# The down product of a gated feed-forward as seven block products in a stage of its own, and gate and up summed in PSUM banks that were read

## The chip, the cores and the metric

One Trainium2 chip, and of it one NeuronCore: TensorE (PE in the profile; its weight loads are PEld), VectorE (DVE), ScalarE (ACT), GpSimd (POOL) and SyncE (SP), which issues the kernel's DMAs. The metric is the device time of one execution in microseconds, the median of the runs shown.

## The reference

A hybrid encoder layer for 1536 tokens (512 of one sequence, 1024 of another) of width 1024: a token mixer, a cross attention to 256 memory rows of each sequence, and a gated feed-forward with a hidden width of 2816, each between RMS norms with a residual. The change lies in the last part:

```python
def swiglu(h, w_gu, w_down):
    gu = h @ w_gu
    gate, up = gu[..., :D_FF], gu[..., D_FF:]
    return (jax.nn.silu(gate) * up) @ w_down
...
    ff = swiglu(rms_norm(x, nw[NORM_PRE_FFN]), ffn_w_gu, ffn_w_down)
    return x + rms_norm(ff, nw[NORM_POST_FFN])
```

## The kernel before, in words

All large products are made in three terms: each fp32 factor is split into a high part and a rest (`split`, L135: ScalarE writes the high part, L136, VectorE the rest, L137), and `mm3` (L156 to L159) issues high x high, high x rest and rest x high into one PSUM bank. Each of these is one matmul with a weight load of its own.

Stages: column products and the mixer (to L518), memory (L521), projections back (L562), cross attention (L662), a second projection (L901), then the feed-forward (L907 to L1040), which the change concerns. The tokens stand in two groups of 768. In a group, gate and up are made for 11 pairs of tiles of the hidden width: `q` counts 44 steps, `g, r = divmod(q, 22)`, `p, up = divmod(r, 2)`; even q are gate, odd q up. Each q is a product of 2x2 blocks in Winograd's form: seven block products (`step` 0 to 6) in place of eight. A block product is four `mm3`, so 12 matmuls of 384 columns. The token side (`S`, seven factors for a group, in the order `NAMES`) stays in SBUF for the whole group; those of the second group wait in DRAM (`sd`) and are loaded and split at q = 21 (L1011 to L1015), through two slots `s_land`.

The weight side of a step is a factor `TS[q, step]`. `load_raw` (L863) loads the weights of a q, `sums` (L871) makes four sums of their blocks on GpSimd, and `make_T` (L882) splits one factor after each product. Five are made ahead; they lie in a ring of five slots, `t_r`.

After each product its PSUM bank is read into SBUF tiles of 384 columns `c[11]`, `c[12]`, `c[21]`, `c[22]` (L973 to L992): one copy by ScalarE (L975) and seven sums by VectorE (L978 to L992; step 5 frees its bank with L989). Every product has a bank of its own from a ring of four (`mm`), and starts it anew. Gate results go through Silu on ScalarE (L995), up results are multiplied by them on GpSimd (L997).

The down product (`down`, L914) is plain and stands among the steps: after steps 2, 4 and 6 of each q from 2 to 41 it takes one tile of 128 tokens of the pair before, 12 matmuls of 512 columns into two `sm` banks, and adds them to `acc` in SBUF (L926, L928). Hidden rows and down weights are split at the end of each up q (L1031 to L1034). `final` (L931) normalises a tile, adds the residual `x2d` and writes it out; the first group's tiles are finished during p = 0 of the second group (L1016 to L1022, L1035). A last loop (L1038) makes the down products of the last two pairs and finishes the second group.

The order on each engine follows the program in the main, but not line by line: the compiler lays out each engine's instructions, and one that is ready can be placed ahead of one that is not. Each engine then runs its own list in that order. All DMAs go through SP's list.

Of the kernel before, what the change touches and what calls it, by code (L numbers as in the profile page):

```python
# [17 lines left out]
P = 128  # L18
# [17 lines left out]
class Part:  # L36
    """Units of a kilo-element per partition in tiles of three units."""
# [30 lines left out]
def carve(units, *specs):  # L68
    """Cut rings of (width, count) out of units, first fit."""
# [13 lines left out]
def encoder_kernel(ctx: ExitStack, tc, x, xTp, xTs, mem, memT, norm_w, w_in, lg, small, sgu_nw, sgu_wT,  # L83
# [72 lines left out]
    def mm3(ps, a, b, first, last):  # L156
        T.matmul(ps, lhsT=a[0], rhs=b[0], start=first, stop=False)  # L157
        T.matmul(ps, lhsT=a[0], rhs=b[1], start=False, stop=False)  # L158
        T.matmul(ps, lhsT=a[1], rhs=b[0], start=False, stop=last)  # L159
# [20 lines left out]
    # Work of one step is emitted in pieces, so that it runs between pieces of the large products.  # L180
# [32 lines left out]
    def xTk(k, t):  # L213
        """hi and lo of x^T (times the norm weight) for k tile k and token tile t."""
# [6 lines left out]
    def load_pairs(src, n):  # L221
        """Two k tiles of a transposed input, times norm weight n."""
# [76 lines left out]
    # the rows of the memory: rsqrt of the mean square, as a column and as a row on all partitions  # L299
# [15 lines left out]
    def chunk_tiles(c, tiles, post):  # L315
        """z of column chunk c for the token tiles; post(i, t, ps) makes the generator that uses it."""
# [22 lines left out]
    # spatial gating  # L339
# [41 lines left out]
    # retention  # L381
# [8 lines left out]
    for h in range(4):  # L390
# [5 lines left out]
        # dec: q forward, k forward, k backward, q backward, whole chunk forward, backward  # L396
# [6 lines left out]
    def ret_tile(h, c, n, t, ps, pk, rf):  # L403
# [5 lines left out]
        # rotary on q and k  # L409
# [160 lines left out]
    def transposed(tiles, n, out, part):  # L570
        """Units of two k tiles: hi and lo of the transposed rows of four token tiles, times norm weight n."""
# [12 lines left out]
    def project(src, w, n_post, res, dst, groups, a_r, xt_r, stat, use, ahead):  # L584
        """dst = res + norm(src^T @ w); use(i, tiles) makes the generator that uses the rows of group i."""
# [541 lines left out]
```

## Time and profile before

| | |
|---|---|
| Time of three runs | 2123.74, 2123.78, 2125.71 us, median 2123.78 |
| Span of the profiled execution | 2124.7 us (no other time of this execution is shown) |
| TensorE busy, share | 98% |
| Feed-forward, first gate matmul to the end | 1088.9 to 2124.7 us |
| Mean granted TensorE clock | 0.996 of full speed |

The span runs from the first to the last instruction; it lies 0.9 us above the median of the runs. Busy times of TensorE are those of pipelined matmuls that overlap, with ends that are modelled, so distances between starts say more. In a timeline row stand the start, the duration, the engine, the line, the operation, out<-in by tile names, the shapes and the count, and in brackets the idle time of the engine before it and what ended it.

### The profile page before, as it was taken

The numbers are of one execution on the slowest core, as the hardware profiler recorded it, in microseconds if no ns is written. First come the engines' busy times: TensorE is split into PE (matmuls) and PEld (weight loads), VectorE is DVE, ScalarE is ACT, GpSimd is POOL, SyncE is SP. The second block draws the span as 40 slices with busy tenths as digits, with TensorE's granted clock in tenths as the row PEclk, the third lists the DMA queues.
The fourth block names the chain that finished last, engine by engine and source line by source line (L and its number), as shares of the span: only waits on it lengthen the run. The fifth ranks groups of instructions, "written<-read, shape, count | busy, mean of one in ns | idle before, by whom it ended". The sixth has DMA issues, their size and how long they took to land.

```text
span 2124.7 us, 28590 instructions
## 1 busy us (share of the span) xinstructions
PE 2087.0 (98%) x10640; PEld 1842.9 (87%) x10640; DVE 1233.0 (58%) x2447; ACT 794.6 (37%) x1588; POOL 565.4 (27%) x537
## 2 busy tenths in 40 slices
PE   8899999999999999999999999999998999999998
PEld 7787888888788888888889999999997999999996
DVE  4235566575423554455666666666678566666666
ACT  7522222234324443444454333333344433333332
POOL 0122222221022200003344233333335433333333
PEclk9999999999999999999999999999999999999999
DMA  8311101024733422243473222122244321221213
GB/s 329 109 39 58 46 16 48 28 66 133 225 102 129 158 71 70 70 139 119 149 212 100 74 76 70 60 70 70 62 160 141 119 70 60 70 70 62 88 50 119
DMA packets 84618, 207.55 MB, mean 98 GB/s; under 512 B 9344, under 2 KB 34560, under 8 KB 84480
## 3 DMA queue, kind: packets, MB, share of 16 engines
q1 hardware_dynamic: 84480, 205.73, 29.7%
q8 instruction: 84, 1.38, 0.3%
q14 instruction: 54, 0.44, 0.1%
HBM read 164.53 MB, written 41.16 MB: 97 GB/s over the span
## 4 chain that ended last, share of the span: by engine, by line
PE 85%; DVE 4%; issue 2%; DMA 2%; POOL 2%; ACT 1%; POOLq 0%; DVEq 0%; ACTq 0%
PE mm L157 17%; PE mm L159 17%; PE mm L158 17%; PE mm L625 12%; PE sm L159 6%; PE sm L158 5%; PE sm L157 5%; POOL rs L172 1%; DVE ra L137 1%; PE sm L578 0%; PE sm L731 0%; PE sm L362 0%; DMA fa<-in_wv_dram 0%; PE sm L818 0%; PE sm L446 0%
## 5 line engine op out<-in xcount | busy, mean ns | idle before, releaser
L136 ACT ACTIVATE ra<-ra 128x512 fp32r<-128x512 f32 x154 | 95.4, 631 | 339.6 <-PE mm L158 180.8
L157 PE MATMUL mm<-rc,ra 128*128 128x384 f32 (+1 forms) x592 | 203.4, 344 | 5.1 <-DVE rb L989 5.1
L158 PE MATMUL mm<-rc,ra 128*128 128x384 f32 (+1 forms) x592 | 202.9, 343 | 0.0
L159 PE MATMUL mm<-rc,ra 128*128 128x384 f32 (+1 forms) x592 | 202.6, 342 | 0.0
L159 PE MATMUL sm<-fb,rb 128*128 128x512 f32 x504 | 199.2, 396 | 1.8 <-DVE rb L137 1.8
L157 PE MATMUL sm<-fb,rb 128*128 128x512 f32 x504 | 196.7, 390 | 1.8 <-ACT fb L136 1.6
L157 PE MATMUL mm<-rx,ra 128*128 128x384 f32 (+1 forms) x512 | 185.1, 362 | 5.9 <-ACT rx L136 5.9
L997 POOL TENSOR_TENSOR rb<-rb 128x384 f32<-128x384 f32 x88 | 116.0, 1337 | 262.0 <-DVE rb L989 207.9
L159 PE MATMUL mm<-rx,ra 128*128 128x384 f32 (+1 forms) x512 | 182.1, 356 | 0.0
L158 PE MATMUL mm<-rx,ra 128*128 128x384 f32 (+1 forms) x480 | 169.0, 352 | 0.0
L136 ACT ACTIVATE ra<-fa 128x512 fp32r<-128x512 f32 (+1 forms) x157 | 100.0, 639 | 150.4 <-PE mm L158 136.8
L137 DVE TENSOR_TENSOR ra<-fa,ra 128x512 fp32r<-128x512 f32 (+1 forms) x157 | 122.4, 779 | 53.0 <-ACT ra L136 52.9
L137 DVE TENSOR_TENSOR ra<-ra,ra 128x512 fp32r<-128x512 f32 x154 | 121.0, 786 | 48.5 <-ACT ra L136 48.5
L157 PEld LDWEIGHTS mm<-rc,ra 128*128 128x128 f32 x592 | 111.8, 189 | 10.0 <-issue 5.9
L158 PEld LDWEIGHTS mm<-rc,ra 128*128 128x128 f32 x592 | 112.0, 189 | 3.5
L159 PEld LDWEIGHTS sm<-fb,rb 128*128 128x128 f32 x504 | 94.8, 188 | 22.8 <-DVE rb L137 2.8
L159 PEld LDWEIGHTS mm<-rc,ra 128*128 128x128 f32 x592 | 111.5, 188 | 2.7
L172 POOL TENSOR_TENSOR rs<-rq,neg_half 128x1 f32<-128x1 f32 x96 | 54.0, 563 | 223.6 <-DVE rq L171 223.6
L157 PEld LDWEIGHTS sm<-fb,rb 128*128 128x128 f32 x504 | 95.0, 188 | 19.4 <-ACT fb L136 1.9
L157 PEld LDWEIGHTS mm<-rx,ra 128*128 128x128 f32 x512 | 97.2, 190 | 12.8 <-ACT rx L136 5.9
L159 PEld LDWEIGHTS mm<-rx,ra 128*128 128x128 f32 x512 | 96.9, 189 | 6.4
L158 PE MATMUL sm<-fb,rb 128*128 128x512 f32 x252 | 100.1, 397 | 0.9 <-DVE fb L137 0.9
(402 smaller groups left out, 5331.4 us busy)
## 6 DMA issues: line engine op xcount, KB each, us to landing
fa<-in_wgu_dram SPq DMA_DIRECT2D x44, 512.0 KB, 3.7
ra<-in_wgu_dram SPq DMA_DIRECT2D x44, 512.0 KB, 4.1
ra<-in_wd_dram SPq DMA_DIRECT2D x44, 512.0 KB, 3.6
fa<-in_w_in_dram SPq DMA_DIRECT2D x20, 512.0 KB, 4.3
fa<-mixT SPq DMA_DIRECT2D x12, 512.0 KB, 3.4
fc<-x1d SPq DMA_DIRECT2D x12, 512.0 KB, 3.8
fa<-oT SPq DMA_DIRECT2D x12, 512.0 KB, 3.3
x2d<-fc SPq DMA_DIRECT2D x12, 512.0 KB, 3.1
```

Source lines behind the costliest of these rows:

```text
L136: A.activation(hi, src, AF.Copy)
L137: V.tensor_tensor(lo, src, f32(hi), op=ALU.subtract)
L157: T.matmul(ps, lhsT=a[0], rhs=b[0], start=first, stop=False)
L158: T.matmul(ps, lhsT=a[0], rhs=b[1], start=False, stop=False)
L159: T.matmul(ps, lhsT=a[1], rhs=b[0], start=False, stop=last)
L172: G.tensor_tensor(out, t, neg_half[:, :w], op=ALU.pow)
L625: T.matmul(pss[i], lhsT=ak[x0], rhs=w[k][x1][:, i * 512 : i * 512 + 512], start=st and k == 0, stop=sp and k == KT - 1)
L997: G.tensor_tensor(c[n], c[n], gated[n], op=ALU.mult)
```

## The change

The seven products of a gate or up step run in another order (A11, A12, S2, S1, S3, A22, S4 on the token side), and three banks serve them. X takes the first, third, fifth and sixth product, one added to the other; ScalarE reads it after the first (r1), third (u2) and fifth (u3), and it is read once more after the sixth. Z takes the fourth and the seventh and is read after each. The second product has a bank of its own. The ring of factors has six slots.

The down product leaves the loop. It becomes a product of 2x2 blocks too (two token halves of a pair of tiles, two tiles of a hidden pair, two halves of the output columns) in seven products. Its left factors, four blocks of the hidden rows and the four sums s1 to s4 of them made by GpSimd (of these eight, seven are kept), are written to DRAM (`hs`) in the gate q that follows. After the loop come 42 units: for each of seven products, six token tiles, with 33 matmuls of 512 columns. The left factor of a unit is loaded from DRAM (two ahead) and split (one ahead); the right factors are quarters of the down weights, loaded again for each product, with differences made on GpSimd, split and kept in 21 slots. Their sums run in four SBUF accumulators. `final` is called in the units of the last two products.

The diff, with removed lines of the loop left out (they stand above), and changes of comments too:

```diff
--- before
+++ after
         split(r, *to)
         return tuple(to)
 
-    def mm3(ps, a, b, first, last):
-        T.matmul(ps, lhsT=a[0], rhs=b[0], start=first, stop=False)
-        T.matmul(ps, lhsT=a[0], rhs=b[1], start=False, stop=False)
-        T.matmul(ps, lhsT=a[1], rhs=b[0], start=False, stop=last)
+    def mm3(ps, a, b, first, last, more=False):
+        T.matmul(ps, lhsT=a[0], rhs=b[0], start=first, stop=False, skip_group_check=more)
+        T.matmul(ps, lhsT=a[0], rhs=b[1], start=False, stop=False, skip_group_check=more)
+        T.matmul(ps, lhsT=a[1], rhs=b[0], start=False, stop=last, skip_group_check=more)
 
     uid = [0]
@@
     TS = {}
-    t_r = Ring(RA.units[3:8])
+    t_r = Ring(RA.units[3:9])
     land = [raw.slots, None]
@@
         G.tensor_tensor(t3, b22, b12, op=ALU.subtract)
         if q > 0:
             sum4(q)
-        queue.extend((q, i, t) for i, t in enumerate((b11, t2, b21, t3, t1, t4, b22)))
+        queue.extend((q, i, t) for i, t in enumerate((b11, b21, t2, t1, t3, t4, b22)))
 
     def make_T():
@@
     sum4(0)
     tmps[0] = nrow[:, 512:D]
     ext = FC.tiles[0]
...
+    s_land = Ring([ext[:, 0 : 4 * HALF], ext[:, 4 * HALF : 8 * HALF]])
+    cs = [t[:, i * HALF : (i + 1) * HALF] for t in (big("rb0", F32), big("rb1", F32), big("rb2", F32))
+          for i in range(8)]
+    gate_r = Ring([cs[0:4], cs[4:8]])
+    up_r = Ring([cs[8:12], cs[12:16]])
+    sum_r = Ring(cs[16:20])
+    cp_r = Ring(cs[20:24])
+    hs = [[dram.tile([3, P, NP, P], F32, tag=f"hs{n}_{g}", name=f"hs{n}_{g}") for g in range(2)] for n in range(7)]
+    def keep(n, g, p, src):
+        nc.sync.dma_start(hs[n - 1][g][:, :, p, :].rearrange("j h t -> h j t"),
+                          src.rearrange("h (j t) -> h j t", t=P))
+    ORDER = (1, 5, 6, 4, 7, 2, 3)
+    units = [(n, tp) for n in ORDER for tp in range(6)]
+    T_tags = deque(["fb", "fc", "rx2", "fd", "ra1", "ra2", "rb0"])
+    T_slots, stash, T2, HS, lands = [], [], {}, {}, {}
+    n_T = [0]
+    def pieces(tag, dtype, w):
+        t = big(tag, dtype)
+        return [t[:, i * w : (i + 1) * w] for i in range(3 * D // w)]
+    def quarter(p, kb, cb, r):
+        nc.sync.dma_start(r, wd[2 * p + kb][:, cb * 512 : (cb + 1) * 512])
+        return r
+    def right(n, p):
+        if n == 1:
+            if p % 6 == 0:
+                stash.extend(pieces(("rx0", "ra0")[p // 6], F32, 512))
+            src = quarter(p, 0, 0, stash[p])
+        else:
+            if 0 not in lands:
+                lands[0] = Ring(pieces("fe", F32, 512))
+            src = lands[0].next()
+            if n in (5, 6, 4):
+                quarter(p, int(n != 5), int(n != 4), src)
+                G.tensor_tensor(stash[p], src, stash[p], op=ALU.subtract)
+                src = stash[p]
             else:
...
+                quarter(p, 1, int(n != 2), src)
+                if n == 7:
+                    o = quarter(p, 0, 1, lands[0].next())
+                    G.tensor_tensor(src, src, o, op=ALU.subtract)
+        i = n_T[0] % 21
+        n_T[0] += 1
+        if i >= len(T_slots):
+            T_slots.extend(pieces(T_tags.popleft(), F32R, D))
+        t = T_slots[i]
+        split(src, t[:, 0:512], t[:, 512:D])
+        T2[n, p] = t
+    def left(i):
+        if i < len(units):
+            if i == 0:
+                t = big("fa", F32)
+                lands["h"] = Ring([t[:, j * NP * P : (j + 1) * NP * P] for j in range(2)])
+            n, tp = units[i]
+            HS[i] = lands["h"].next()
+            nc.sync.dma_start(HS[i], hs[n - 1][tp // 3][tp % 3].rearrange("h p t -> h (p t)"))
+    def left_split(i):
+        if i < len(units):
+            if i == 0:
+                lands["s"] = Ring([(t[:, 0 : NP * P], t[:, NP * P : 2 * NP * P])
+                                   for t in (big("rc2", F32R), big("rc1", F32R))])
+            o = lands["s"].next()
+            split(HS[i], *o)
+            HS[i] = o
+    def prepare(step):
+        if step == 3:
+            left(0)
+            left(1)
+        if step >= 3:
+            for p in range((step - 3) * 3, min((step - 2) * 3, NP)):
+                right(1, p)
+        if step == 4:
+            left_split(0)
+    NG = 2 * 2 * NP
+    LEFT = ("A11", "A12", "S2", "S1", "S3", "A22", "S4")
+    out_q = deque()
+    for q in range(NG):
+        g, r = divmod(q, 2 * NP)
+        p, up = divmod(r, 2)
+        c = up_r.next() if up else gate_r.next()
+        c11, c12, c21, c22 = c
+        for step in range(7):
+            u = TS.pop((q, step))
+            name = LEFT[step]
+            if step == 0:
+                X = ps = mm()[:, 0:HALF]
+            elif step == 1:
+                ps = mm()[:, 0:HALF]
+            elif step == 3:
+                Z = ps = mm()[:, 0:HALF]
+            else:
+                ps = Z if step == 6 else X
+            for k in range(4):
+                b = [v[:, k * HALF : (k + 1) * HALF] for v in S[name]]
+                a = u[:, k * P : (k + 1) * P], u[:, 512 + k * P : 512 + (k + 1) * P]
+                mm3(ps, a, b, step in (0, 1, 3) and k == 0, k == 3, step not in (0, 1, 3))
+            advance()
+            if step == 0:
+                r1 = cp_r.next()
+                A.activation(r1, X, AF.Copy)
+            elif step == 1:
+                V.tensor_tensor(c11, r1, ps, op=ALU.add)
+            elif step == 2:
+                u2 = cp_r.next()
+                A.activation(u2, X, AF.Copy)
+            elif step == 4:
+                u3 = cp_r.next()
+                A.activation(u3, X, AF.Copy)
+                V.tensor_tensor(c22, u3, Z, op=ALU.add)
+            elif step == 5:
+                if up:
+                    V.tensor_tensor(c21, gated[2], X, op=ALU.mult)
+                else:
+                    A.activation(c21, X, AF.Silu)
+            elif step == 6:
+                V.tensor_tensor(c12, u2, Z, op=ALU.add)
+            n = {1: 0, 4: 3, 6: 1}.get(step)
+            if n is not None:
+                if up:
+                    G.tensor_tensor(c[n], c[n], gated[n], op=ALU.mult)
+                else:
+                    A.activation(c[n], c[n], AF.Silu)
+            if step == 0 and q + 1 < NG:
+                load_raw(q + 1)
+            if step == 2 and q + 1 < NG:
+                sums(q + 1)
+            make_T()
+            if out_q and step in (2, 3, 4, 5):
+                out_q.popleft()()
+            if q == NG - 1:
+                prepare(step)
+            if r == 2 * NP - 1 and g == 0:
+                t = s_land.next()
+                nc.sync.dma_start(t, sd[name].rearrange("p k t -> p (k t)"))
+                split(t, *S[name])
+        if not up:
+            gated = c
+        else:
+            def tail(c, g, p):
+                h11, h12, h21, h22 = c
+                s1, s2, s3, s4 = (sum_r.next() for _ in range(4))
+                def one():
+                    G.tensor_tensor(s1, h21, h22, op=ALU.add)
+                    G.tensor_tensor(s3, h11, h21, op=ALU.subtract)
+                def two():
+                    G.tensor_tensor(s2, s1, h11, op=ALU.subtract)
+                    keep(1, g, p, h11)
+                    keep(4, g, p, h22)
+                def three():
+                    G.tensor_tensor(s4, h12, s2, op=ALU.subtract)
+                    keep(2, g, p, h12)
+                    keep(5, g, p, s1)
+                    keep(7, g, p, s3)
+                def four():
+                    keep(6, g, p, s2)
+                    keep(3, g, p, s4)
+                return one, two, three, four
+            out_q.extend(tail(c, g, p))
+    while out_q:
+        out_q.popleft()()
+    accs = {}
+    def acc(n, tp):
+        if n not in accs:
+            accs[n] = big({"c11": "rc0", "c22": "rx1", "c21": "rb1", "c12": "rb2"}[n], F32)
+        return accs[n][:, tp * 512 : (tp + 1) * 512]
+    out = {}
+    def final(t, a, fast):
+        if not out:
+            o = pieces("ra0", F32, 512)
+            out["f"] = o[0:2]
+            for i in range(2):
+                nc.sync.dma_start(o[i], norm_w[POST_FFN][i * 512 : (i + 1) * 512].partition_broadcast(P))
+            out["j"] = Ring(o[2:6])
+            out["x"] = Ring(pieces("rx0", F32, D))
+        xt = out["x"].next()
         nc.sync.dma_start(xt, x2d[t])
         sq = tiny(2, "sq2")
         for i in range(2):
...
+            A.activation(out["j"].next(), a[i], AF.Square, accum_out=sq[:, i : i + 1])
         rs = tiny(1, "rs1")
         rms_of(sq, rs)
         dst = out_p[t * P : (t + 1) * P, :] if t < 4 else out_s[(t - 4) * P : (t - 3) * P, :]
         for i in range(2):
             s = slice(i * 512, i * 512 + 512)
...
+            V.scalar_tensor_tensor(a[i], a[i], rs, out["f"][i], op0=ALU.mult, op1=ALU.mult)
+            (G if i == 0 and not fast else V).tensor_tensor(a[i], a[i], xt[:, s], op=ALU.add)
+            nc.sync.dma_start(dst[:, s], a[i])
+    for ui, (n, tp) in enumerate(units):
+        then = ORDER[ORDER.index(n) + 1] if n != ORDER[-1] else None
+        left(ui + 2)
+        left_split(ui + 1)
+        ps = (mm if ui % 2 else sm)()
+        h = HS.pop(ui)
+        for p in range(NP):
+            t = T2[n, p]
+            mm3(ps, [q[:, p * P : (p + 1) * P] for q in h], (t[:, 0:512], t[:, 512:D]), p == 0, p == NP - 1)
+            if then and p in (2, 6):
+                k = 2 * tp + (p == 6)
+                if k < NP:
+                    right(then, k)
+        c11, c12, c21, c22 = (acc(m, tp) if n != 1 or m == "c11" else None for m in ("c11", "c12", "c21", "c22"))
+        if n == 1:
+            A.activation(c11, ps, AF.Copy)
+        elif n == 5:
+            A.activation(c22, ps, AF.Copy)
+        elif n == 6:
+            V.tensor_tensor(c21, c11, ps, op=ALU.add)
+            G.tensor_tensor(c12, c22, c21, op=ALU.add)
+        elif n == 4:
+            V.tensor_tensor(c21, c21, ps, op=ALU.add)
+        elif n == 7:
+            V.tensor_tensor(c22, c12, ps, op=ALU.add)
+            V.tensor_tensor(c21, c21, ps, op=ALU.add)
+        elif n == 2:
+            V.tensor_tensor(c11, c11, ps, op=ALU.add)
+            final(PAIRS[tp][1], (c21, c22), False)
+        else:
+            V.tensor_tensor(c12, c12, ps, op=ALU.add)
+            final(PAIRS[tp][0], (c11, c12), tp == 5)
 def _tables():
```

## Rows read from the trace of the kernel before

**Rows 1.** The page, busy time of TensorE, share of the span, instructions.

```profile
PE 2087.0 (98%) x10640; PEld 1842.9 (87%) x10640; DVE 1233.0 (58%) x2447; ACT 794.6 (37%) x1588; POOL 565.4 (27%) x537
```

**Rows 2.** Windows: stretch, length, busy time by engine, clock, DMA share, GB/s.

```profile
1127.00:1560.00 433.00, 432.18 (x2259) 402.42 (x2258) 275.57 (x425) 148.29 (x259) 150.56 (x116) 1.00 0.22 69
...
1630.00:1640.00 10.00, 5.69 (x25) 5.40 (x24) 7.72 (x14) 2.49 (x6) 5.34 (x5) 0.83 0.49 159
...
2075.00:2080.00 5.00, 5.00 (x31) 5.00 (x30) 2.75 (x5) 1.59 (x2) 1.01 (x1) 1.00 0.80 246
```

**Rows 3.** Timeline of TensorE, starts that bound the feed-forward and its steps.

```profile
1088.91 0.33 PE L157 MATMUL mm<-rc,ra 128*128 128x384 f32 x1
...
1168.81 0.33 PE L157 MATMUL mm<-rc,ra 128*128 128x384 f32 x1
...
1191.73 0.33 PE L157 MATMUL mm<-rc,ra 128*128 128x384 f32 x1
...
2066.95 0.33 PE L157 MATMUL mm<-rc,ra 128*128 128x384 f32 x1
...
2081.51 0.39 PE L157 MATMUL sm<-fb,rb 128*128 128x512 f32 x1
...
2085.29 0.39 PE L157 MATMUL sm<-fb,rb 128*128 128x512 f32 x1
...
2115.01 0.39 PE L159 MATMUL sm<-rc,rc 128*128 128x512 f32 x1
```

**Rows 4.** Timeline of TensorE around 1635 us, a long wait and its end.

```profile
1635.27 0.66 PE L157 MATMUL mm<-rc,ra 128*128 128x384 f32 x1 [4.31 <-DVE rb L989]
...
1638.56 0.33 PE L158 MATMUL mm<-rc,ra 128*128 128x384 f32 x1
```

**Rows 5.** Timeline, a bank's last matmul, its reader, and a matmul that waits.

```profile
1107.63 0.54 DVE L989 TENSOR_TENSOR rb<-rb,mm 128x384 f32<-128x384 f32 x1
1107.67 0.34 PE L159 MATMUL mm<-rc,ra 128*128 128x384 f32 x1
...
1108.32 0.41 PE L157 MATMUL mm<-rc,ra 128*128 128x384 f32 x1 [0.31 <-DVE rb L989]
...
1108.57 0.34 PE L158 MATMUL mm<-rc,ra 128*128 128x384 f32 x1
...
1834.13 0.33 PE L159 MATMUL mm<-rx,ra 128*128 128x384 f32 x1
...
1834.50 0.55 DVE L983 TENSOR_TENSOR rb<-rb,mm 128x384 f32<-128x384 f32 x1 [1.42 <-PE mm L159]
```

**Rows 6.** Line 975, ScalarE's copy of a bank: ns min/median/max, first and last start.

```profile
L975 ACT ACTIVATE rb<-mm x44: 463/472/491, 1091.7 to 2071.7; 128x384 f32<-128x384 f32 x44
```

**Rows 7.** Timeline of TensorE in the mixer, order on the engine.

```profile
271.19 0.39 PE L450 MATMUL sm<-fe,fb 128*128 128x128 f32 x2
271.33 0.49 PE L157 MATMUL mm<-rx,ra 128*128 128x512 f32 x1
271.65 0.27 PE L424 MATMUL sm<-ident,fe 128*128 128x128 f32 x1
```

**Rows 8.** Lines 869 and 997 in 1160 to 1560 us, GpSimd's sums and gatings.

```profile
L869 POOL TENSOR_TENSOR fa<-ra x9: 1292/1296/1303, 1182.1 to 1547.9; 128x512 f32<-128x512 f32 x9
...
L997 POOL TENSOR_TENSOR rb<-rb x35: 1010/1429/1478, 1164.8 to 1533.9; 128x384 f32<-128x384 f32 x35
```

**Rows 9.** Timelines of SP, ScalarE and VectorE, one token factor at q = 21.

```profile
1577.03 0.32 SPq L1014 DMA_DIRECT2D fc<-sdA  x1
...
1582.93 1.49 ACT L136 ACTIVATE fd<-fc 128x1536 fp32r<-128x1536 f32 x1 [1.69 <-DMA fc<-sdA]
...
1584.46 1.76 DVE L137 TENSOR_TENSOR fd<-fc,fd 128x1536 fp32r<-128x1536 f32 x1 [0.67 <-ACT fd L136]
```

**Rows 10.** Timeline of the end, VectorE's second sum of the last tile.

```profile
2116.42 0.68 DVE L928 TENSOR_TENSOR rb<-rb,sm 128x512 f32<-128x512 f32 x1
```

More of the change, by code (lines that the diff above doesn't have):

```diff
@@ L907, in encoder_kernel @@
     ext = FC.tiles[0]
-    hidden = RB.tiles[0]
-    cs_r = Ring([t[:, i * HALF : (i + 1) * HALF] for t in [big("rb1", F32)] for i in range(8)])
-    acc = [u for t in (big("rb2", F32), big("rx0", F32)) for u in Part([t]).units]
-    wds = []
-    tiles_of = [[PAIRS[3 * g + i][j] for j in range(2) for i in range(3)] for g in range(2)]
-    def down(first, pos, terms):
-        ps = [sm(), sm()]
-        n = 2 * len(terms)
-        for i in range(2):
-            for j in range(n):
-                hidden, w = terms[j // 2]
-                o = (j % 2) * 4 * HALF + pos * P
-                a = hidden[:, o : o + P], hidden[:, 2 * HALF + o : 2 * HALF + o + P]
-                mm3(ps[i], a, [q[:, i * 512 : i * 512 + 512] for q in w[j % 2]], j == 0, j == n - 1)
-        for i in range(2):
-            s = acc[pos][:, i * 512 : i * 512 + 512]
-            if first:
-                A.activation(s, ps[i], AF.Copy)
-            else:
-                V.tensor_tensor(s, s, ps[i], op=ALU.add)
-        return ps
@@ L931, in final @@
-    def final(g, pos, x_r, last):
-        t = tiles_of[g][pos]
-        a = acc[pos]
-        xt = x_r.next()
+    s_land = Ring([ext[:, 0 : 4 * HALF], ext[:, 4 * HALF : 8 * HALF]])
[6 more added lines that the diff above has]
+    hs = [[dram.tile([3, P, NP, P], F32, tag=f"hs{n}_{g}", name=f"hs{n}_{g}") for g in range(2)] for n in range(7)]
@@ L937, in final @@
         for i in range(2):
-            j = jk_r.next()
-            A.activation(j, a[:, i * 512 : i * 512 + 512], AF.Square, accum_out=sq[:, i : i + 1])
+            A.activation(out["j"].next(), a[i], AF.Square, accum_out=sq[:, i : i + 1])
         rs = tiny(1, "rs1")
@@ L944, in final @@
             s = slice(i * 512, i * 512 + 512)
-            V.scalar_tensor_tensor(a[:, s], a[:, s], rs, frow[:, s], op0=ALU.mult, op1=ALU.mult)
-            (G if i == 0 and not last else V).tensor_tensor(a[:, s], a[:, s], xt[:, s], op=ALU.add)
-            nc.sync.dma_start(dst[:, s], a[:, s])
-    frow = ext[:, 0:D]
-    x_r = Ring([ext[:, D : 2 * D]])
-    jk_r = Ring([ext[:, 2 * D : 2 * D + 512], ext[:, 2 * D + 512 : 3 * D]])
-    s_land = Ring([ext[:, 0 : 4 * HALF], ext[:, 4 * HALF : 8 * HALF]])
@@ L1037, in encoder_kernel @@
-    x_r = Ring([x_r.slots[0]] + Part([big("rx1", F32)]).units)
-    for pos in (3, 4, 5, 0, 1, 2):
-        down(False, pos, [(hidden, wds), (into, w)])
-        final(1, pos, x_r, pos == 2)
+            V.scalar_tensor_tensor(a[i], a[i], rs, out["f"][i], op0=ALU.mult, op1=ALU.mult)
[33 more added lines that the diff above has]
+            final(PAIRS[tp][0], (c11, c12), tp == 5)
```

79 lines of the change are left out of this document (removed).

## The prediction, before the change was run

> **What bounds the kernel now.** I read the page first: TensorE is busy for 2087.0 us, 98% of the span [rows 1]. So only fewer matmuls, or fewer waits, can shorten the kernel. Next I cut the feed-forward part into windows: between 1127 and 1560 us TensorE's mark never leaves full clock, while VectorE has 275.6 us of work in 433, ScalarE 148.3 and GpSimd 150.6, and the DMA share is 0.22 [rows 2]. The other engines have room there. Then I read TensorE's own timeline, because busy times of pipelined matmuls overlap and only distances between starts add up. The feed-forward part runs from 1088.91 to its last matmul at 2115.01, 1026.1 us [rows 3]. A step pair of the loop (seven block products and three pieces of the down product) takes 1191.73 - 1168.81 = 22.92 us; one without down pieces takes 2081.51 - 2066.95 = 14.56 us [rows 3]. The closing down products, alone on the engine, start every (2115.01 - 2085.29)/131 = 0.227 us [rows 3].
>
> **The sum for before.** 44 q of 14.56 us are 640.6 us. 40 of them carry three down pieces: 40 x 8.36 = 334.4. The last 144 down matmuls take 33.7 (2081.51 to 2115.01 and one interval). Sixteen transposes add about 1.6. That is 1010.3 of 1026.1 us; the other 15.8 us are waits, two thirds of them around 1635 to 1646 us, where TensorE waits 4.31 us at once for VectorE's sums and then restarts slowly [rows 4].
>
> **The change, part by part.**
>
> *Down product.* Before, 2 groups x 11 pairs x 6 tiles x 12 = 1584 matmuls of 512 columns. After, 7 products x 6 token tiles x 11 x 3 = 1386. They no longer stand between gate and up products, so I price them all at 0.227: 314.6 us in place of 334.4 + 33.7 = 368.1. **Gain 53.5 us.** This is the largest term, and it lies wholly on TensorE.
>
> *Gate and up.* The same 84 matmuls for each q, so 640.6 us stay. New is that X is added to after it was read. Step 2 adds to X after copy r1, which has the whole of step 1 as cover; step 4 likewise has step 3; step 6 adds to Z after VectorE's c22, which has step 5. Only step 5 follows step 4 on the same bank with nothing in between: ScalarE's copy u3 must end first, and all later matmuls stand behind the one that waits. Its price, if nothing fills it: a reader starts 0.37 us after the last matmul starts (1834.13 to 1834.50), the copy takes 0.47 [rows 5, 6], and after a reader's end (1107.63 + 0.54) the matmul starts 0.15 us later, its successor 0.25 after that instead of 0.17 [rows 5]. 0.37 + 0.47 + 0.15 - 0.17 + 0.08 = **0.90 us for each q**, 39.6 us for 44. That would eat most of the gain.
>
> But engine order is not program order in this kernel. At 271.33 one matmul of the next column product (L157) stands ahead of transposes that the program issues first and whose input was late; TensorE does not wait [rows 7]. The same can happen here: when u3 is due, step 0 of the next q needs only a free bank, S["A11"] and a factor prepared five steps ahead, so its matmuls can stand in the gap. Five of them (6 x 0.17 > 0.99) cover it, four leave about 0.12 and the slower restart. Bounds are 0 and 0.90; I take 0.2, since the row shows fillers placed one at a time and so a rest below about one matmul. **Cost 44 x 0.2 = 8.8 us.**
>
> *Other engines during gate and up.* VectorE loses four sums for each q, the down sums and all splits of hidden rows; seven splits and three or four sums are left, under 7 us in 14.6. ScalarE gets two more copies of 0.47 us and loses the same splits. GpSimd has for a pair of q eight sums of 1.3, three gatings and four new sums of 1.43 [rows 8]: 20.4 us in about 30, down from nothing that limits; five steps of lead cover its delays. The factor ring has six slots for five, which can only loosen. Costed at nothing; if the lead were gone, each late factor would show as a TensorE wait.
>
> *SyncE.* Seven new writes for each pair of q stand in its queue behind GpSimd's sums. Behind them waits the weight load of the next gate q. GpSimd ends the last of these sums some 13 us into the gate q (one gating 1.4, four sums 5.2, four new sums 5.7, after about 1 us of lead); the load then needs to land in the up q before its step 2 ends, 14.6 + 3 x 2.08 = 21 us in. There are some 7 us of room for the transfer. Nothing on the path.
>
> *Second group's tokens (q = 21).* Seven loads through two slots. A turn of a slot is the transfer (issue 1577.03, used 1582.93: 5.9), ScalarE's 1.49 and VectorE's 1.76 [rows 9], some 9 us with gaps, so a factor every 4.5 us. Before, a product with a down piece left 3.3 us each; now 2.1. The seventh lands some 29 to 31 us after the first product, and step 6 of q = 22 asks for it at 12 x 2.08 = 25. **6 us** (bounds 0 and 13, the latter if the copies of X also stand behind these splits on ScalarE).
>
> *Start and transitions.* The opening q share ScalarE with the tokens of group two: 3 us (0 to 6). From q = 43 to the down stage: right and left factors of the first units are made inside q = 43, 3 us (0 to 6).
>
> *Supply of the down stage.* The loads of down weights move here from the up steps: 88 of 0.26 MB for 44 of 0.52, the same bytes; so do all twelve reads of the residual and the final steps. One unit is 33 x 0.227 = 7.5 us. It needs 0.72 MB of left factors and about two quarters of 0.26 MB; with the residual read and the result written (n = 2) it is 2.2 MB, 290 GB/s. The window at 2075 moved 246 GB/s at a share of 0.80 [rows 2], 307 at a full share. So one product of seven is near the limit. GpSimd, ScalarE and VectorE each have under 5 us of work in 7.5. **2 us** (0 to 15).
>
> *Gone with the old order:* the late final steps of group one and their 11 us of waits; they are in the 15.8 us that I don't carry over. *End:* one sum after the last matmul instead of two, and the second began 1.4 us after the last matmul started [rows 10]: 1 us less.
>
> **Sum.** 640.6 + 314.6 + 1.6 + 8.8 + 6 + 3 + 3 + 2 = 979.6 against 1026.1; with the end, 47.5 us less. From the profiled span of 2124.7 that is 2077.2; the runs' median is 0.9 below that span, so on their scale about **2077 us**, 2.2% faster. About 0.2% is what a measurement can tell from no change.
>
> **The rivals.**
>
> *The gap stays open.* The order could leave step 5 right behind step 4. For it: program order, and each wait of this kind in the old trace is paid in full [rows 5]. Against: the fillers of rows 7. Price: 44 x (0.90 - 0.2) = 30.8 us more, 2108 us. Still faster. Chance 0.15.
>
> *The pauses cost the clock.* If the gap stays open, TensorE pauses 44 times. After the pause of 4.31 us at 1635.27 the granted clock of its window fell to 0.83 and ten matmuls took 1638.56 - 1635.27 = 3.29 us instead of 1.73 [rows 2, 4], a drop to the lower level of 1.2 GHz. If each open gap did that, it would cost 1.56 us on top: 44 x 1.56 = 69 us, 2108 + 69 = 2177 us, **slower** by 2.5%. It decides from some ten such drops on (2108 is 16 us below before). Against: the wait at 1107.67, of 0.31 us idle, was followed by a normal 0.25 and no slow matmul [rows 5]. The Trainium skill, "TensorE: Matmul & The Clock Gate", section "A second HAM failure mode: psum-queue depth-cycling", tells of just this: small idles between groups while cycling through PSUM banks made the clock swing between its levels. By that rule the time would be the 2177 above; the trace so far speaks against it. Chance 0.06.
>
> *The DRAM way binds.* If the left factors come later than their units, or the token change and the transitions cost their upper bounds (15 + 13 + 6 + 6 in place of 14), 26 us more: 2103 us. For it: 290 GB/s for one product. Against: two loads in flight, each with 7.5 us. Chance 0.07. *The products gain nothing:* had the added traffic and both of the first costs come together (30.8 and 26 more than forecast), the time would be 2134 us: no gain; chance 0.03, half of it within 0.2%.
>
> **How the numbers follow.** The forecast has 0.69: its own range is 2062 (no rest in the gap, no cost at the token change, 14.8 less) to 2095. With the open gap and the DRAM case the range goes to 2112. Faster: 0.69 + 0.15 + 0.07 = 0.91, less 0.04 for several mishaps at once; slower 0.08; same 0.05.
>
> **What would show it.** Right: starts of 512-column matmuls 0.227 apart in one block of some 317 us at the end; in the gate and up stage a q every 14.6 to 14.9 us, with a few matmuls of the next step 0 ahead of step 5; a pause of several us near q = 21 or 22. The open gap would show as a wait of the step 5 matmul for ScalarE's copy, 44 times some 0.8 us, and a q of 15.5 us. The clock rival would show slices below 1.00 through the gate stage. Supply would show as TensorE waiting for the splits of left factors late in the down stage. The forecast is wrong if a q takes over 15.2 us, or the down stage over 330.

## The result, and the profile after

The kernel after takes 2093.97 us (median of four runs, 2092.86 to 2094.58) where the one before takes 2123.76 in the same session: ratio 0.9859, 95% interval 0.9845 to 0.9872, **29.8 us or 1.4% faster**. The forecast was 2077, 47 us faster. So the sign held, the range too, by 1 us at its slow end, and 17 us of the gain are missing. The profiled execution took 2094.58 us with a span of 2092.8. Where differences between experiments are given, they come from their ratios to the kernel before, times 2124, since that kernel itself moved by 2 us between sessions.

The page of the kernel after, sums by engine and TensorE's clock (before: [rows 1]):

```profile
PE 2048.4 (98%) x10442; PEld 1806.6 (86%) x10442; DVE 1168.0 (56%) x2088; ACT 843.5 (40%) x1651; POOL 755.9 (36%) x653
...
PEclk9999999999999999999999999999999999899999
```

TensorE is as full as before, on fewer matmuls. One clock slice late in the run is below full. The windows find it (before: [rows 2]; length, busy time by engine, clock, DMA share, GB/s):

```profile
1127.00:1410.00 283.00, 283.00 (x1609) 277.99 (x1608) 169.10 (x201) 126.31 (x233) 197.46 (x145) 1.00 0.39 119
1755.00:1790.00 35.00, 29.83 (x122) 23.95 (x121) 24.58 (x16) 11.57 (x16) 30.23 (x19) 0.90 0.70 230
1790.00:1850.00 60.00, 55.11 (x233) 45.10 (x232) 28.74 (x18) 19.12 (x25) 33.34 (x21) 0.94 0.57 182
1850.00:2080.00 230.00, 230.00 (x1016) 190.54 (x1015) 140.37 (x163) 82.30 (x123) 47.04 (x37) 1.00 0.55 185
...
1810.00:1820.00 10.00, 5.49 (x25) 4.21 (x23) 10.00 (x6) 1.86 (x2) 10.00 (x7) 0.92 0.42 127
```

From 1127 to 1410 us and in the last 230 us TensorE is full, at full clock. The first 95 us of the down stage are not: there VectorE does few instructions in much time (six in 10 us in the last line), beside a GpSimd that is busy throughout. TensorE's timeline, kernel after (before: [rows 3, 5, 7]):

```profile
1125.68 0.34 PE L157 MATMUL mm<-rc,ra 128*128 128x384 f32 x1
...
1140.48 0.34 PE L157 MATMUL mm<-rc,ra 128*128 128x384 f32 x1
...
1312.45 0.34 PE L159 MATMUL mm<-rx,ra 128*128 128x384 f32 x1
1312.62 0.33 PE L157 MATMUL mm<-rc,ra 128*128 128x384 f32 x1
...
1313.49 0.34 PE L159 MATMUL mm<-rc,ra 128*128 128x384 f32 x1
1313.77 0.44 PE L157 MATMUL mm<-fd,ra 128*128 128x384 f32 x1
1314.05 0.33 PE L158 MATMUL mm<-fd,ra 128*128 128x384 f32 x1
...
1755.47 0.39 PE L158 MATMUL sm<-fb,rc 128*128 128x512 f32 x1
...
1780.20 0.50 PE L157 MATMUL mm<-fb,rc 128*128 128x512 f32 x1 [2.99 <-ACT rc L136]
1783.11 0.79 PE L159 MATMUL mm<-fb,rc 128*128 128x512 f32 x1 [2.18 <-DVE rc L137]
...
1820.38 0.79 PE L159 MATMUL mm<-fd,rc 128*128 128x512 f32 x1 [4.89 <-DVE rc L137]
...
2083.95 0.39 PE L159 MATMUL mm<-ra,rc 128*128 128x512 f32 x1
```

Three readings. A q takes 1140.48 - 1125.68 = **14.80 us**, 0.24 over the 14.56 without a wait. Six matmuls of the next q's step 0 (1312.62 to 1313.49, factor rc) stand between step 4 (rx) and step 5 (fd): the fillers that the prediction hoped for. The down stage, 1755.47 to 2083.95 and one interval, takes 328.7 us for work of 313.7: **15 us of waits**, in units 2, 3 and 7 of 42, counted from 0 (10.63, 12.23 and 14.99 us for 7.48), for splits of left factors (rc). The rest behind the last matmul is 8.85 us where it was 9.7, as forecast.

Not all of these 15 us are idle time: the three waits shown make 10.1. The rest is clock. Rows of TensorE and windows, kernel after:

```profile
1105.10 0.69 PE L157 MATMUL mm<-fd,ra 128*128 128x384 f32 x1 [1.93 <-ACT rb L1028]
...
1431.00 0.44 PE L157 MATMUL mm<-rx,ra 128*128 128x384 f32 x1 [1.49 <-ACT rb L1025]
...
1784.13 0.63 PE L158 MATMUL mm<-fb,rc 128*128 128x512 f32 x1
...
1787.55 0.49 PE L157 MATMUL mm<-fc,rc 128*128 128x512 f32 x1
```

```profile
1105.20:1108.40 3.20, 3.20 (x10) 3.20 (x11) 2.45 (x5) 0.52 (x1) 0.62 (x1) 0.50 0.75 207
1432.90:1436.00 3.10, 3.10 (x11) 3.10 (x11) 3.10 (x3) 1.01 (x2) 3.10 (x3) 0.50 0.87 236
1781.00:1787.70 6.70, 4.59 (x11) 3.62 (x12) 6.70 (x4) 2.53 (x4) 6.70 (x5) 0.50 0.52 177
1818.60:1825.30 6.70, 4.92 (x12) 3.86 (x13) 4.94 (x3) 0.00 (x0) 5.45 (x3) 0.50 0.58 182
```

In each of these four stretches, which follow or hold a wait of TensorE, the granted clock is 0.50, the lower level of 1.2 GHz. From 1784.13 to 1787.55 eight matmuls start 0.43 us apart instead of 0.227. In the first two stretches, in the opening q and in the token change, some ten matmuls start 0.32 us apart instead of 0.17; an estimate from these starts is 1.5 us for each.

What the reader of X does at 1312, ScalarE's timeline:

```profile
1312.70 0.63 ACT L136 ACTIVATE ra<-fa 128x512 fp32r<-128x512 f32 x1 [1.42 <-PE mm L158]
1313.24 0.47 ACT L1028 ACTIVATE rb<-mm 128x384 f32<-128x384 f32 x1
```

The copy u3 (L1028) starts 0.79 us after step 4's last matmul, not 0.37: the same matmuls free a slot for a factor's split (L136), which goes first.

What VectorE does in the down stage, kernel after, groups of instructions of 1755 to 1850 us (busy us, mean ns, idle before), with GpSimd's differences:

```profile
L137 DVE TENSOR_TENSOR rc<-fa,rc 128x1408 fp32r<-128x1408 f32 x10 | 19.4, 1943 | 36.1 <-ACT rc L136 36.1
...
L137 DVE TENSOR_TENSOR fc<-rx,fc 128x512 fp32r<-128x512 f32 x3 | 5.2, 1784 | 0.0
...
L950 POOL TENSOR_TENSOR rx<-fe,rx 128x512 f32<-128x512 f32 x18 | 29.4, 1664 | 4.6 <-DMA fe<-in_wd_dram 4.6
```

and its timeline just ahead of the wait at 1820.38:

```profile
1805.77 5.20 DVE L137 TENSOR_TENSOR fc<-rx,fc 128x512 fp32r<-128x512 f32 x3
...
1817.65 2.68 DVE L137 TENSOR_TENSOR rc<-fa,rc 128x1408 fp32r<-128x1408 f32 x1
```

A row of right-factor splits (fc, rx, fd) at some 1.75 us each stands ahead of the left factor's (rc). The first wait, at 1780.20, is for ScalarE's part of a left split; in ScalarE's list that part stands behind parts of right factors that wait for a difference of GpSimd (L950):

```profile
1778.25 0.63 ACT L136 ACTIVATE rb<-ra 128x512 fp32r<-128x512 f32 x1 [1.04 <-POOL ra L950]
1778.78 1.36 ACT L136 ACTIVATE rc<-fa 128x1408 fp32r<-128x1408 f32 x1
```

**Theory:** VectorE and GpSimd slow each other when both run, and left splits queue behind the slow right ones, which are bunched at the stage's start. **Rivals:** the left factors come late from DRAM; GpSimd's differences are awaited, without slowing anything; the order alone costs.

### The profile page after: what moved, and what is told of

Read it like the earlier page. It is cut to its first block, busy times and chain, and to the rows that moved or that the text cites. A ratio compares the mean times of both kernels' runs of the same rounds, so it can differ in the third digit from the quotient of the medians.

```text
span 2092.8 us, 28421 instructions
## 1 busy us (share of the span) xinstructions
PE 2048.4 (98%) x10442; PEld 1806.6 (86%) x10442; DVE 1168.0 (56%) x2088; ACT 843.5 (40%) x1651; POOL 755.9 (36%) x653
## 4 chain that ended last, share of the span: by engine, by line
PE 86%; DVE 3%; DMA 2%; issue 2%; POOL 2%; ACT 1%; SPq 0%; DVEq 0%; POOLq 0%; ACTq 0%
PE mm L157 20%; PE mm L159 20%; PE mm L158 20%; PE mm L625 12%; PE sm L157 3%; PE sm L158 3%; PE sm L159 3%; PE sm L731 1%; PE sm L578 0%; PE sm L362 0%; PE sm L446 0%; PE sm L450 0%; DVE rc L137 0%; DMA fa<-in_wv_dram 0%; PE sm L818 0%
## 5 line engine op out<-in xcount | busy, mean ns | idle before, releaser
L137 DVE TENSOR_TENSOR ra<-ra,ra 128x512 fp32r<-128x512 f32 x155 | 170.8, 1103 | 122.0 <-ACT ra L136 121.9
L137 DVE TENSOR_TENSOR ra<-fa,ra 128x512 fp32r<-128x512 f32 (+1 forms) x157 | 146.2, 933 | 62.8 <-ACT ra L136 61.7
L136 ACT ACTIVATE ra<-fa 128x512 fp32r<-128x512 f32 (+1 forms) x157 | 100.8, 643 | 166.9 <-PE mm L158 142.4
L136 ACT ACTIVATE ra<-ra 128x512 fp32r<-128x512 f32 x155 | 97.8, 631 | 152.4 <-PE mm L158 98.4
L136 ACT ACTIVATE rc<-fa 128x1408 fp32r<-128x1408 f32 (+1 forms) x54 | 70.7, 1309 | 193.4 <-PE sm L158 70.6
L137 DVE TENSOR_TENSOR rc<-fa,rc 128x1408 fp32r<-128x1408 f32 (+1 forms) x50 | 84.9, 1699 | 58.1 <-ACT rc L136 58.1
L415 POOL TENSOR_TENSOR fe<-fe,fb 128x128 f32<-128x128 f32 x96 | 51.3, 555 | 180.2 <-DVE fe L407 173.9
L157 PEld LDWEIGHTS mm<-rx,ra 128*128 128x128 f32 x512 | 97.1, 190 | 13.5 <-ACT rx L136 5.9
L159 PEld LDWEIGHTS mm<-rx,ra 128*128 128x128 f32 x512 | 97.1, 190 | 6.3
L158 PEld LDWEIGHTS mm<-rx,ra 128*128 128x128 f32 x480 | 90.9, 189 | 5.2 <-DVE rx L137 0.8
L593 POOL TENSOR_TENSOR rx<-fa,rx 128x1024 fp32r<-128x1024 f32 x6 | 14.5, 2411 | 211.3 <-PE sm L731 190.2
L157 PE MATMUL mm<-rx,rb 128*128 128x512 f32 x208 | 88.3, 425 | 0.1
```

The lines of the kernel that those rows point to most:

```text
L136: A.activation(hi, src, AF.Copy)
L137: V.tensor_tensor(lo, src, f32(hi), op=ALU.subtract)
L157: T.matmul(ps, lhsT=a[0], rhs=b[0], start=first, stop=False, skip_group_check=more)
L158: T.matmul(ps, lhsT=a[0], rhs=b[1], start=False, stop=False, skip_group_check=more)
L159: T.matmul(ps, lhsT=a[1], rhs=b[0], start=False, stop=last, skip_group_check=more)
L415: G.tensor_tensor(t2q[:, s], zq[:, 1 - s], sinT[:, o : o + 64].unsqueeze(1).broadcast_to([P, 2, 64]), op=ALU.mult)
```

## The experiments

**Differences on VectorE.**

```
-                G.tensor_tensor(stash[p], src, stash[p], op=ALU.subtract)
+                V.tensor_tensor(stash[p], src, stash[p], op=ALU.subtract)
...
-                    G.tensor_tensor(src, src, o, op=ALU.subtract)
+                    V.tensor_tensor(src, src, o, op=ALU.subtract)
```

> The differences of down weights (33 of products 5, 6, 4 and 11 of product 7) go from GpSimd to VectorE. Theory (in the first three units of the down stage the splits of left factors stand in VectorE's queue behind splits of right factors that wait for GpSimd's differences, and both engines slow each other: a 512-column split takes 1.55 to 1.79 us there instead of 0.69): splits go back to about 0.7 us, a right factor costs VectorE 1.4 us instead of waiting 1.73 for GpSimd, and 6 to 12 of the 15 us of waits of the down stage go: 2082 to 2088 us. Rival (the left factors come late from DRAM): unchanged, 2092 to 2096 us, with the waits where they were. Rival (VectorE becomes the bound): over 2096 us.

Measured: 2079.55 us, ratio 0.9782 (0.9767 to 0.9796), 16 us less than the kernel after and 2.5 below the range expected. The same groups, in this kernel:

```profile
L137 DVE TENSOR_TENSOR rc<-fa,rc 128x1408 fp32r<-128x1408 f32 x12 | 19.4, 1620 | 15.5 <-ACT rc L136 15.5
...
L137 DVE TENSOR_TENSOR fc<-rx,fc 128x512 fp32r<-128x512 f32 x3 | 1.9, 684 | 0.0
...
L950 DVE TENSOR_TENSOR rx<-fe,rx 128x512 f32<-128x512 f32 x18 | 11.4, 683 | 8.6 <-DMA fe<-in_wd_dram 8.6
```

With GpSimd idle a split takes 684 ns in place of 1784, and a difference 683 on VectorE in place of 1664 on GpSimd. VectorE has 35 operations more in this stretch (18, 15 and 2) and is less late. Of TensorE's waits in the stage one of 1.16 us is left, and the clock stays at 1.00 there. DRAM traffic is the same, so the DRAM rival falls. That GpSimd's differences were awaited is not told apart from interference by this run; the next one tests interference by itself.

**GpSimd busy for nothing.** The same kernel, with GpSimd working beside VectorE.

```
+                if n in (5, 6):
+                    if "junk" not in lands:
+                        lands["junk"] = big("rb2", F32)[:, 0:512]
+                    G.tensor_tensor(lands["junk"], src, src, op=ALU.subtract)
                 V.tensor_tensor(stash[p], src, stash[p], op=ALU.subtract)
```

> As with all differences on VectorE (2079.55 us), and GpSimd makes a difference of the same size for each down weight of products 5 and 6, that nobody uses. VectorE no longer waits for GpSimd, but both are busy at once. If the two slow each other (interference): VectorE's 512-column splits and differences of that time take 1.3 us or more instead of 0.68, and several us of waits come back in the first units, 2083 to 2092 us. If only the order in the queues and the wait for GpSimd's result cost time: splits stay at 0.68 to 0.75 us and the time at 2078 to 2081 us.

Measured: 2096.25 us, ratio 0.9860 (0.9845 to 0.9874): all 16 us are gone again, and the time is 4 us above the range expected. Its groups, a wait of TensorE, and VectorE beside GpSimd, whose eleven operations end at 1785.64; its next starts at 1789.12:

```profile
L137 DVE TENSOR_TENSOR rc<-fa,rc 128x1408 fp32r<-128x1408 f32 x10 | 18.7, 1869 | 10.3 <-ACT rc L136 10.3
L954 DVE TENSOR_TENSOR rx<-fe,rx 128x512 f32<-128x512 f32 x18 | 18.1, 1049 | 8.3 <-DMA fe<-in_wd_dram 8.2
```

```profile
1788.38 0.80 PE L159 MATMUL mm<-fb,rc 128*128 128x512 f32 x1 [5.26 <-DVE rc L137]
```

```profile
1768.83 16.81 POOL L953 TENSOR_TENSOR rb<-fe 128x512 f32<-128x512 f32 x11 [4.98 <-DMA fe<-in_wd_dram]
...
1784.67 1.52 DVE L954 TENSOR_TENSOR rx<-fe,rx 128x512 f32<-128x512 f32 x1
1786.11 0.68 DVE L954 TENSOR_TENSOR ra<-fe,ra 128x512 f32<-128x512 f32 x1
```

VectorE's splits and differences use nothing that GpSimd makes, and the differences take 1049 ns in place of 683. Within this run, between 1755 and 1850 us, VectorE's operations on two SBUF operands of 512 columns take 675 to 694 ns where no operation of GpSimd stands beside them (32 of them) and 1429 to 1527 where one does for nine tenths of their time or more (15). That is interference, shown, and it costs 16 us by itself. One path remains beside it: GpSimd's reads hold the landing slots longer. But VectorE's wait for loads ahead of its rx differences is 8.3 us here and 8.6 without GpSimd's work, so that path adds nothing in this group. The waits of TensorE stand in units 2 to 5 here, not in 2, 3 and 7. So the run does not tell how the 15 us of the kernel after divide between slow operations and differences that are awaited.

**Right factors paced.** GpSimd keeps its work, the order in the queues is changed.

```
+    def after(r):
+        hi, lo = newest[0]
+        V.tensor_tensor(r[:, 0:2], f32(hi[:, 0:2]), f32(lo[:, 0:2]), op=ALU.add)
+        return r
...
-            src = lands[0].next()
+            src = after(lands[0].next())
```

> Each load of a down weight for products 5 to 3 is tied to the newest split left factor (VectorE writes two columns of the landing slot from it), so right factors can no longer be bunched in the first units of the stage and no left split stands behind more than two or three of them. GpSimd keeps the differences. Theory (the order in VectorE's queue is what costs): 8 to 13 of the 15 us of waits of the down stage go, 2081 to 2086 us, and splits take about 0.7 us mostly. Rival (GpSimd is too slow in itself, whatever the order): a part of the waits stays in each unit, 2090 us or more. Rival (DRAM supply): loads start later than now, so more waits, over 2096 us.

Measured: 2086.53 us, ratio 0.9813 (0.9799 to 0.9828), 10 us less than the kernel after. Behind the first unit, which is shared with the last q, 17 units take 7.48 us each; the wait that is left is later, for a right factor (fb). That wait, and the group of splits shown above for the other kernels:

```profile
1900.61 0.69 PE L157 MATMUL sm<-fb,rc 128*128 128x512 f32 x1 [2.15 <-ACT fb L136]
```

```profile
L137 DVE TENSOR_TENSOR fc<-rx,fc 128x512 fp32r<-128x512 f32 x3 | 2.9, 966 | 3.8 <-ACT fc L136 3.8
```

So the order in the queues, with GpSimd still making the differences, is enough to take the waits out of units 2, 3 and 7. But spread out, the splits are faster too, 966 ns for 1784: the run takes away the bunching and much of the slowness together. The first run, where the same row of splits stands ahead of a left factor (1795 to 1801 us), shows that the order costs little while the splits are fast; whether slow splits would cost TensorE without bunching is not shown.

**Left factors read twice.**

```
             nc.sync.dma_start(HS[i], hs[n - 1][tp // 3][tp % 3].rearrange("h p t -> h (p t)"))
+            nc.sync.dma_start(HS[i], hs[n - 1][tp // 3][tp % 3].rearrange("h p t -> h (p t)"))
```

> Each left factor of the down stage is read from DRAM twice, the second time over the first: 42 loads of 0.72 MB more, 30 MB. Theory (queue order and interference of VectorE and GpSimd): two loads of about 4.2 us still fit in the 15 us that a landing slot has, the stage gets 0 to 4 us longer: 2094 to 2098 us. Rival (DRAM supply is what the stage waits for): the waits of units 2 and 3 and those near product 2 grow by a load each and later units wait too, 15 us or more: 2109 us or more.

Measured: 2096.40 us, ratio 0.9861 (0.9845 to 0.9878): no change, with the DMA share at 0.81 to 0.85 through the stage instead of 0.55 to 0.70. Units 2, 3 and 7 get shorter (9.18, 8.14, 8.61 us) and other units get waits of 0.2 to 2.2. Later loads also spread the right factors, so the run does not give the clean price of a load. But 30 MB more do not cost the 15 us that supply would.

**Two banks, no fillers.** With step 1 in Z no matmul of the next q may start early.

```
+    X, Z = mm()[:, 0:HALF], mm()[:, 0:HALF]
     for q in range(NG):
...
+            ps = Z if step in (1, 3, 6) else X
```

> One bank X and one bank Z for all gate and up products; step 1 uses Z. Then no matmul of the next q is free to stand between step 4 and step 5, and nothing fills the time of the copy u3. Theory: the gap stands open in full, 43 times. By the rows of the kernel after (last matmul of step 4 at 1312.45, step 5 at 1313.77, less the normal 0.17, and 0.1 for the restart) the rest is 1.25 us instead of 0.24, a q takes 15.8 us, 43 us more: 2137 us; by the prediction's 0.90 us a q takes 15.46 us, 28 us more: 2122 us. Rival (the pauses cost the clock): each adds some 1.56 us, 2180 us or more, with a granted clock below 1.00 through the gate stage. Rival (the six fillers save nothing): 2092 to 2096 us.

Measured: 2145.31 us, ratio 1.0092 (1.0077 to 1.0107): **slower than before**, 50 us more than the kernel after and 8 more than the rows gave. Its timeline and a window:

```profile
1312.38 0.44 PE L157 MATMUL mm<-fd,ra 128*128 128x384 f32 x1 [0.98 <-ACT rb L1022]
...
1328.19 0.44 PE L157 MATMUL mm<-fd,ra 128*128 128x384 f32 x1 [0.98 <-ACT rb L1022]
```

```profile
1127.00:1410.00 283.00, 265.35 (x1505) 259.60 (x1504) 141.36 (x189) 117.53 (x216) 176.13 (x135) 1.00 0.37 111
```

A q takes 15.81 us: an open gap costs 1.25 us, not 0.90. The six fillers decide the sign of the whole change. The clock stays at 1.00 through pauses of 0.98 us in each q, so the clock rival falls for pauses of this length.

**Step 5 in its own bank.**

```
+            elif step == 5:
+                ps = mm()[:, 0:HALF]
...
-                if up:
-                    V.tensor_tensor(c21, gated[2], X, op=ALU.mult)
-                else:
-                    A.activation(c21, X, AF.Silu)
+                V.tensor_tensor(c21, u3, ps, op=ALU.add)
...
-            n = {1: 0, 4: 3, 6: 1}.get(step)
+            n = {1: 0, 4: 3, 5: 2, 6: 1}.get(step)
```

> Step 5 of the gate and up products gets a bank of its own, and VectorE adds it to the copy u3; c21's Silu and its product with the gate are then made as for the other three blocks (ScalarE, GpSimd). No matmul waits for u3. Theory (the rest of 0.24 us in each q is all that adding on in banks that were read still costs): a q takes 14.56 us, 43 x 0.24 = 10 us less: 2084 us. Rival (the rest comes from elsewhere, or VectorE's added sum gives it back): 2091 to 2097 us.

Measured: 2110.06 us, ratio 0.9925 (0.9910 to 0.9939), 14 us **more** and outside both ranges expected. Every second q does take 14.57 us, so the rest of 0.24 is the wait at step 5. The others take 15.36. Timelines of VectorE and TensorE:

```profile
1318.90 1.47 DVE L137 TENSOR_TENSOR ra<-fa,ra 128x512 fp32r<-128x512 f32 x1 [1.20 <-ACT ra L136]
1320.30 0.54 DVE L1031 TENSOR_TENSOR rb<-rb,mm 128x384 f32<-128x384 f32 x1
...
1320.89 0.44 PE L157 MATMUL mm<-fe,ra 128*128 128x384 f32 x1 [0.50 <-DVE rb L1031]
```

Step 6 now waits for c22's sum (L1031), which stands behind a split that took 1.47 us. Without its pause TensorE is at step 6 before VectorE is, and no filler stands there. The split itself is slow beside a sum of GpSimd. The wait moved, with interest. Of the 14 us, 9 lie in the gate and up stage (with its start and the token change) and 5 in the down stage.

**Both of these.** Differences on VectorE and step 5 in its own bank.

> Differences of down weights on VectorE, and step 5 in its own bank. The two are in different stages, so the gains add: 14.4 us as measured for the first and 10 us by theory for the second, 2069 to 2071 us. If the second gives nothing: 2079 to 2080 us.

Measured: 2093.18 us, ratio 0.9842 (0.9826 to 0.9859), well above both figures expected. The down stage kept its gain, the gate stage its loss; the expectation rested on the theory that the run before this one refuted.

**u3 on VectorE.** The gap stays, its length changes.

```
-                A.activation(u3, X, AF.Copy)
+                V.tensor_copy(u3, X)
```

> The copy u3 goes from ScalarE to VectorE; banks and sums stay as in the kernel after. In the rows of that kernel u3 starts 0.79 us after the last matmul of step 4, since ScalarE makes a split of 0.63 us first, and five to seven matmuls of the next step 0 stand in the gap. Theory (that split ahead of u3 makes the rest of 0.24): u3 starts some 0.4 us after the matmul, takes about 0.55, and the fillers cover it: a q takes 14.56 to 14.65 us, 6 to 10 us less: 2084 to 2088 us. Rival (VectorE is late too, behind its own splits, or slowed by GpSimd): a q takes 14.8 us or more, 2093 us or more.

Measured: 2087.00 us, ratio 0.9820 (0.9803 to 0.9836), 8 us less. A q takes 14.61 us. TensorE and VectorE:

```profile
1311.37 0.33 PE L159 MATMUL mm<-rx,ra 128*128 128x384 f32 x1
1311.54 0.34 PE L157 MATMUL mm<-rc,ra 128*128 128x384 f32 x1
...
1312.23 0.34 PE L158 MATMUL mm<-rc,ra 128*128 128x384 f32 x1
1312.41 0.38 PE L157 MATMUL mm<-fd,ra 128*128 128x384 f32 x1
```

```profile
1311.74 0.56 DVE L1028 COPY rb<-mm 128x384 f32<-128x384 f32 x1 [0.81 <-PE mm L159]
```

The copy starts 0.37 us after the last matmul, the prediction's own figure, and five fillers cover it.

**u3 and the differences on VectorE.**

> u3 and the differences of down weights on VectorE. Gate stage and down stage don't share a wait, so the gains add: 2079.6 less what u3 on VectorE alone gives, 2070 to 2074 us by theory; 2079 us or more if that gives nothing.

Measured: **2071.54 us** (2071.09 to 2073.09), ratio 0.9750 (0.9735 to 0.9764): the two gains add, and this version beats both kernels, by 2.5% and 1.1%.

**Four landing slots at q = 21.**

```
-    s_land = Ring([ext[:, 0 : 4 * HALF], ext[:, 4 * HALF : 8 * HALF]])
+    more = big("fb", F32)
+    s_land = Ring([t[:, i * 4 * HALF : (i + 1) * 4 * HALF] for t in (ext, more) for i in range(2)])
```

> The left factors of the second group's tokens (q = 21) land in four slots instead of two. Theory (the turn of two slots sets the pace of the seven factors, as the prediction had it): of the 7.4 us that the token change costs TensorE 4 to 7 go, 2087 to 2090 us. Rival (the factors wait behind other work in the queues of SyncE and ScalarE, not for a slot): unchanged, 2092 to 2096 us.

Measured: 2097.48 us, ratio 0.9866 (0.9851 to 0.9881): no gain. The seven factors are split earlier, and TensorE then waits for VectorE's sums and splits instead (1.14, 3.37 and 1.31 us).

**One group of tokens.** The loads and splits at q = 21 are left out, so the second group is computed from the first group's factors and its outputs are not those of the layer.

```
-            if r == 2 * NP - 1 and g == 0:
+            if False:
```

> The seven loads and splits of the second group's left factors at q = 21 are left out; the second group is computed from the first group's factors. All matmuls stay. Theory (the trace's own account of the token change, 7.4 us over three q): q = 21, 22 and 23 take 14.8 us like the others, 6 to 9 us less: 2085 to 2088 us. Rival (part of that loss is something else at the change of group): 2089 us or more.

Measured: 2089.04 us, ratio 0.9829 (0.9813 to 0.9846), 6 us less, and q = 21 to 23 take 14.80 us each. The median lies just in the rival's range (2089 us or more), the ratio, which stands for 2087.4 us in the session of the result, in the theory's; the q settle it. That is the price of the token change, 7.5 us in the trace.

## Why the prediction was right in sign and 17 us short

*Matmuls.* Right. The down stage is one block at 0.227 us a matmul, 313.7 us of work for 314.6 forecast, and a q without waits takes 14.57.

*The gap at step 5.* Rest 0.24 us for 0.2: right in size, and by the mechanism named, fillers from the next q. But two errors nearly cancel, and that is luck: the gap is 1.25 us, not 0.90 (the addend 0.37 is 0.79, since ScalarE makes a split first), and there are six fillers, not five. So the rival of the open gap was priced wrongly by 20 us (30.8 forecast, 50 measured, of which 43 x 1.01 are the gaps themselves, 3.7 a longer token change and 2.4 the down stage). With the gap alone put right (44 x 1.25) that rival comes to 2123 us, no change; measured, it was 20 us slower than before. Its chance of 0.15 was counted as faster.

*The clock rival.* Refuted for the gaps that it named. The Trainium skill's section "A second HAM failure mode: psum-queue depth-cycling" in "TensorE: Matmul & The Clock Gate" tells of a clock that swings with such small idles; here 0.98 us of idle in each q left the granted clock at 1.00. But what the rival feared did happen in the kernel after, at other waits: after 1.93 us of idle in the opening q, behind a wait of 1.49 us in the token change, and at the waits of the down stage the granted clock was 0.50. By the estimates above this is 1.5 + 1.5 + 5 = 8 of the missing 17 us. The sum has no term for it: it priced waits at their idle time outside this rival.

*Token change.* 6 us forecast, 7.5 in the trace, some 1.5 of them lower clock. The price was near and its cause was not the turn of two slots: four gain nothing. The waits are for a copy and a split of ScalarE (1.49 and 1.84 us) and a split of VectorE (0.62), whose queues hold the seven splits and the sums of the products together; that this is the cause is argued, not shown.

*Start.* 3 us forecast, 5.7 in the trace; not tested. The wait of 1.93 us for u3 in the opening q and the slow matmuls behind it are some 3.4 of them.

*The down stage's supply.* This is the step that failed, a term that was mis-sized. "GpSimd, ScalarE and VectorE each have under 5 us of work in 7.5", 2 us, with 3 more for the transition: 5 forecast, 15 and 1.2 measured, 11 of the missing 17. In the stage's first 35 us GpSimd is busy for 30.2 and VectorE for 24.6, which is 6.5 and 5.3 us in 7.5. The sum looked for the danger in DRAM, and took two things for granted: that an operation of VectorE costs the same beside a busy GpSimd, and that each unit's work is done in that unit. The runs showed both to be false. Bunched splits cost 1.75 us, and a left factor stands behind them. Some 10 of the 15 us are idle time, some 5 the lower clock. The upper bound of 15 was met, by another mechanism.

The terms that missed: 1.5 (gap) + 1.5 (tokens) + 2.7 (start) + 11.2 (supply and transition) - 0.9 (down matmuls) = 16.0 of the 16.6 us by which the feed-forward part is over its forecast (996.2 for 979.6). The forecast itself is rounded up: 2077.2 less 0.9 is 2076.3.

## What to carry to other kernels

Price an operation that reads two operands from SBUF on VectorE, or on GpSimd, by rows in which the other engine is busy too, and move differences to where the splits are made rather than to the idle engine. Where a matmul adds onto a bank that was just read, look at what stands ahead of the reader in its engine's queue and at which independent matmuls may fill the gap; those decided here between 1.4% faster and 0.9% slower. Price a pause of TensorE with the slow matmuls that can follow it: in the down stage 10.1 us of idle cost 15. A wait taken away by a new operation can come back one step later, as the own bank for step 5 showed.

## What was not expected of the hardware

A VectorE operation on two SBUF operands of 128x512 takes 0.68 us beside an idle GpSimd and up to 1.8 beside a busy one, and GpSimd's own operation of that size goes from 1.30 [rows 8] to a mean of 1.66. One that reads a bank and one SBUF operand is not touched. In the kernel after, c22's sum, over all 44 q (ns min/median/max, first and last start):

```profile
L1029 DVE TENSOR_TENSOR rb<-rb,mm x44: 539/547/549, 1106.5 to 1751.3; 128x384 f32<-128x384 f32 x44
```

From 1127 to 1410 us GpSimd is busy 197 of 283 us. Of VectorE's 384-column sums of a bank and an SBUF operand in the feed-forward, the 103 with GpSimd at work for nine tenths of their time or more take 541 to 555 ns, the 31 without any 539 to 555. The Trainium skill has this rule, in "SBUF — State Buffer", section "Who interferes with whom": a VectorE instruction with two SBUF inputs contends with a GpSimd instruction that reads SBUF, one with at most one such input, outside VectorE's 2-port performance modes, does not. The trace agrees on both sides, with 0.68 to 1.78 us for the first and 539 to 549 ns for the second.
